# Rotary query rows reach main memory in whole tiles and are put in order there; head sums, head outputs and loads change their places

## The chip, the cores and the metric

One core of a Trainium2 chip runs the whole program. The metric is the device time of one execution in microseconds, taken over repeated executions (median). The profile shown is of one further execution.

## What is computed

Two layers of an encoder for 1024 positions of width 1024, float32. Each layer has, side by side, multi-head latent attention (8 heads, 64 plain and 32 rotary dimensions per query and key, values of 64) and a convolution module of 512 channels with 31 taps; then an output product, and a gated feed-forward part with its own short convolution. Cut to what matters:

```python
q = (c_q @ w_uq[l]).reshape(b, s, MLA_HEADS, MLA_NOPE_DIM + MLA_ROPE_DIM)
q_rope = _apply_rope(q[..., MLA_NOPE_DIM:], cos_h, sin_h)
sc = einsum("bqhd,bkhd->bhqk", qn, k_nope) + einsum("bqhr,bkr->bhqk", qr, k_rope)
p = softmax(sc * scale); o = einsum("bhqk,bkhd->bqhd", p, v)
u = silu(layernorm(dwconv(a * sigmoid(gt))))
x = x + concat([y_attn, u]) @ w_o[l]
x = x + (silu(zg) * zv) @ w_down[l]
```

## The kernel before

Everything lies transposed: features on the 128 partitions, the 1024 positions along the free axis. Numbers are held as pairs (an upper and a lower part), so that a product is three matmuls or, for the scores, matmuls over stacked parts in 16-bit floats.

`project` (L564) makes latents, keys and queries of one layer. TensorE's order is the list `seq`; each section's eviction is a generator, and a small model of the clock (`work`, `launch`, `finish`) decides where its steps are placed on VectorE and ScalarE. Rotary queries come out as two tiles of 128 rows (8 heads by 16 rows): i = 0 the first halves, i = 1 the second halves, each split in an upper part p = 0 and a lower part p = 1 (`query_rope`, L772). Head 0 (`DIRECT`) gets its rows straight from there, by transfers within on-chip memory. The other heads go through main memory: `qd` and `kd` hold plain queries and keys, `qrd` and `krd` the rotary ones, `qrd[p, h]` being the 32 rows of one head in order. `query_rope` appends its spills to the list `spills` (L797), 16 rows and one part each; `query` (L799) empties the list on SyncE's queue from the second block of heads on, with its own spill of `qd` at the end.

`load_head` (L782) loads a head's three tiles by twelve transfers on SyncE's queue: `q` (plain rows, then rotary rows twice), `k` (both parts, the upper part again, the rotary rows), and `qc`, four copies of the lower rotary rows, in a tile that two heads share. `key` (L755) does the same for head 0's keys.

`attention` (L1795) goes over 64 query tiles n = 8 h + qt, two at a time (a pair; the loop at L2059). In each pair TensorE makes products of probabilities and values (`products`, `values`, L1894), the scores of the next pair (`begin`, `scores`, L1825: four matmuls over plain and rotary parts at L1836, and four small ones with `qc` at L1843), and transposes of the present pair's probabilities (`turn`, L1873; the evictions are `upper` on ScalarE and `lower` on VectorE). VectorE takes the largest score of each row (L1854), ScalarE the exponentials (L1862). The load of head h + 1 is put on the queue in the second pair of head h; that of head 1 in the second pair of head 0.

All other work is in `agenda`, a list per step n that `others(n)` runs: `others(n)` in the middle of a pair, `others(n + 1)` at its end. There are the convolution taps on GpSimd (`tap_late`, L2133: a product, then mostly a transfer that accumulates), the totals of the convolution (`conv_total`, from step `TOTAL_TIME` = 57), loads of the output weights (`ahead`: step 55, additions in steps 58 to 61, four more loads in step 61), and the heads' ends. When the last values of a head are through (n = 8 h + 11), the reciprocals of its sums are taken (`inverses`), and `sums` (L1933) is appended to step n + 1: a transpose on TensorE, a copy on ScalarE, and two transfers on SyncE that spread the row over partitions (`rb`). For an odd head `sums` appends the product of the outputs with `rb` on GpSimd (L1944, step 8 h + 10 + `Y_DELAY`) and, `Y_SPLIT` or for head 5 `Y_LAST` steps later, the split of the outputs in two parts (L1946: a cast on ScalarE at L224, a subtraction on GpSimd at L226). Behind the last pair but one `early` (L1959) multiplies these parts with the output weights (L1034), heads 1, 3 and 5 first.

Of the kernel before, what the change touches and what calls it, by code (L numbers as in the profile page):

```python
# [12 lines left out]
F16 = mybir.dt.float16  # L13
# [5 lines left out]
T = 1024  # L19
D = 1024  # L20
DEPTH = 2
HEADS = 8
NOPE = 64
ROPE = 32
HALF = ROPE // 2
# [39 lines left out]
FFN_BANKS = (2, 4)  # L65
SIDE_TIME = 56
TOTAL_TIME = 57
Y_DELAY = 6
Y_LAST = 4
Y_SPLIT = 8  # L70
LATE_FROM = 0
# [70 lines left out]
class Encoder:  # L142
# [421 lines left out]
    def project(self, l, carry):  # L564
# [4 lines left out]
        gates, ckv, kvs, cq, cqs, vs, w = {}, [], [], [], [], [], {}  # L569
        heads, pending, spills = {}, {}, []  # L570
        qd = self.dp.tile([HEADS, NOPE, 2, T], F16, name=f"qd{l}")
        qrd = self.dp.tile([2, HEADS, ROPE, T], F16, name=f"qrd{l}")
        kd = self.dp.tile([HEADS, NOPE, 2, T], F16, name=f"kd{l}")
        krd = self.dp.tile([2, ROPE, T], F16, name=f"krd{l}")
# [4 lines left out]
        st = {}  # L579
# [175 lines left out]
        def key(j):  # L755
            if j == 0:
                heads.update((h, self.head_tiles(l, h)) for h in range(DIRECT))
            p = ps[f"k{j}"]
            hl = self.blk(f"ks{l}_{j}", F16, (128, 2, T))
            nc.scalar.activation(out=hl[:, 0], in_=p, func=AF.Copy, scale=col(6))  # L760
            yield 0.0, 0.0
            nc.vector.scalar_tensor_tensor(out=hl[:, 1], in0=p, scalar=col(6), in1=hl[:, 0], op0=ALU.mult, op1=ALU.subtract)
            self.move(kd[2 * j:2 * j + 2].rearrange("h d p t -> (h d) p t"), hl)
            for h in range(DIRECT if j == 0 else 0):
                k, mine = heads[h][1], hl[h * NOPE:(h + 1) * NOPE]
                for p in range(2):
                    self.move(k[p * NOPE:(p + 1) * NOPE, 0], mine[:, p])
                    self.move(k[NOPE + p * ROPE:NOPE + (p + 1) * ROPE, 1], krd[p])
                self.move(k[0:NOPE, 1], mine[:, 0])
            yield 1.22, 0.0  # L770

        def query_rope(i):  # L772
            p = ps[f"u{i}"]
            c, s = self.blk(f"rc{l}_{i}"), self.blk(f"rs{l}_{i}")
            nc.vector.tensor_tensor(out=c, in0=p, in1=st["cos"], op=ALU.mult)
            nc.vector.tensor_tensor(out=s, in0=p, in1=st["sin"], op=ALU.mult)
            st["rope", i] = c, s
            yield 2.44, 0.0
            if i == 0:
                return  # L780
            (c1, s1), (c2, s2) = st.pop(("rope", 0)), st.pop(("rope", 1))
            nc.vector.tensor_tensor(out=c1, in0=c1, in1=s2, op=ALU.subtract)  # L782
            nc.vector.tensor_tensor(out=c2, in0=c2, in1=s1, op=ALU.add)
            two = [self.blk(f"qr{l}_{i}", F16, (128, 2, T)) for i in range(2)]
            for hl, o in zip(two, (c1, c2)):
                nc.scalar.copy(out=hl[:, 0], in_=o)
            yield 2.5, 1.0
            for i, (hl, o) in enumerate(zip(two, (c1, c2))):
                nc.vector.scalar_tensor_tensor(out=hl[:, 1], in0=o, scalar=1.0, in1=hl[:, 0], op0=ALU.mult, op1=ALU.subtract)
                yield 1.25, 0.0  # L790
                for h in range(DIRECT):
                    for r, (t, p) in enumerate([(heads[h][0][:, 1], 0)] * 2 + [(heads[h][2][:, h % 2], 1)] * 4):
                        at = i * HALF + (NOPE + r * ROPE if p == 0 else (r - 2) * ROPE)
                        self.move(t[at:at + HALF], hl[h * HALF:(h + 1) * HALF, p])
                for p in range(2):
                    for h in range(HEADS):
                        spills.append((qrd[p, h, i * HALF:(i + 1) * HALF], hl[h * HALF:(h + 1) * HALF, p]))  # L797

        def query(j):  # L799
            n = self.blk(f"qn{l}_{j}")  # L800
# [76 lines left out]
        times, starts, t = {}, {}, 0.0  # L877
# [904 lines left out]
    def load_head(self, l, h, qd, qrd, kd, krd, kc):  # L1782
        q, k, qc = tiles = self.head_tiles(l, h)
        self.move(q[0:NOPE], qd[h])
        self.move(q[NOPE:128, 0], qd[h][:, 0])
        for p in range(2):
            self.move(k[p * NOPE:(p + 1) * NOPE, 0], kd[h][:, p])
            self.move(q[NOPE + p * ROPE:NOPE + (p + 1) * ROPE, 1], qrd[0, h])
        self.move(k[0:NOPE, 1], kd[h][:, 0])
        self.move(k[NOPE:128, 1], krd.rearrange("p d t -> (p d) t"))  # L1790
        for r in range(4):
            self.move(qc[r * ROPE:(r + 1) * ROPE, h % 2], qrd[1, h])
        return tiles

    def attention(self, l, u, conv, away, spill, kvs, loaded, ahead, wo, begun):  # L1795
# [4 lines left out]
        state, v, vts = {}, [], {}  # L1800
# [93 lines left out]
        def values(group, c, n):  # L1894
            h, gg = divmod(group, 2)
            st = state[h]
            e = h % 2
            main, aux = slice(e * 64, e * 64 + 64), slice(64 - e * 64, 128 - e * 64)
            if c == 0:
                if gg == 0 and e == 0:  # L1900
                    st["y"], st["rb"] = self.blk(f"yt{l}_{h}"), self.blk(f"rb{l}_{h}")
                elif gg == 0:
                    st["y"], st["rb"] = state[h - 1]["y"], state[h - 1]["rb"]
                st["po", gg] = self.bank(f"o{l}_{h}_{gg}")
            y, rb, po = st["y"], st["rb"], st["po", gg] if c < 3 else st.pop(("po", gg))
            pt = st["pt"][gg][c // 2]
            for i in range(2):
                nc.tensor.matmul(po, v[2 * c + i][:, h // 2, e, :], pt[0][:, 2 * (c % 2) + i, :],  # L1908
                                 start=(c == 0 and i == 0), stop=False, skip_group_check=True)
            if c == 3:  # L1910
                for kt in range(8):
                    rows = slice(kt % 2 * 64, kt % 2 * 64 + 64)
                    nc.tensor.matmul(po[rows], v[kt][:, h // 2, e, main], st["pt"][gg][kt // 4][1][:, kt % 4, :],
                                     start=False, stop=(kt >= 6), skip_group_check=True)
            if c < 3:
                return
            st["pt"].pop(gg)
            qs = HALVES[gg]
            nc.scalar.activation(out=y[main, qs], in_=po[aux, :], func=AF.Copy, scale=vr[aux, 0:1])
            nc.vector.scalar_tensor_tensor(out=y[main, qs], in0=po[main, :], scalar=vr[main, 0:1], in1=y[main, qs], op0=ALU.mult, op1=ALU.add)  # L1920
            if h < HEADS - 2 and gg:
                inverses(h)
                agenda[n + 1].append(lambda: sums(h, main, st, y, rb))
            elif h == HEADS - 1:
                if gg:
                    divide(y[main, qs], main, gg)
                else:
                    agenda[n + 1].append(lambda: (divide(y[main, qs], main, gg), finish(last, y, 0)))
# [46 lines left out]

        ys, inv, po = [], {}, begun["po"]
        total = HEADS * 8
        agenda = defaultdict(list)
        late, rest = [], {j: list(away[j]) for j in range(4)}
        while any(rest.values()):  # L1980
            j = max((j for j in rest if rest[j]), key=lambda j: (all(j != e for e, _ in late[-2:]), len(rest[j]), -j))
# [16 lines left out]
        last = HEADS - 1  # L1998
        state_y = lambda: state[last]["y"]
        agenda[55].append(lambda: inverses(last - 1))  # L2000
        agenda[56].append(lambda: sums(last - 1, slice(0, 64), state[last - 1], state[last - 1]["y"], state[last - 1]["rb"]))
        agenda[60].append(lambda: [self.load_y(l, begun["x"], 0, k) for k in range(2)])
        for c, when in enumerate((60, 62)):
            agenda[when].append(lambda c=c: inv.update({c: inverse(c)}))
# [15 lines left out]
        def products(n):  # L2020
            for g, c in chain.get(n, ()):
                values(g, c, n)
# [35 lines left out]
        others(0)  # L2058
        for pair in range(total // 2 - 1):  # L2059
            n, nxt = 2 * pair + 1, pair + 1  # L2060
            products(n)
            begin(nxt)
            turn(pair, 0)
            upper(pair, 0)
            turn(pair, 1)
            upper(pair, 1)
            largest(2 * nxt)
            ends = [rows(tt) for tt in ROWS_LATE.get(n, ())]
            turn(pair, 3)
            upper(pair, 3)  # L2070
            second.pop(nxt)()
            lower(pair, 0)
            largest(2 * nxt + 1)
            expo(2 * nxt)
            lower(pair, 1)
            for f in ends:
                f()
            others(n)
            products(n + 1)
            ends = [rows(tt) for tt in ROWS_LATE.get(n + 1, ())]  # L2080
            turn(pair, 2)
            upper(pair, 2)
            expo(2 * nxt + 1)
            lower(pair, 2)
            lower(pair, 3)
            for f in ends:
                f()
            others(n + 1)
            for qi in range(2):
                state[pair // 4]["p"].pop(2 * (pair % 4) + qi)  # L2090
# [198 lines left out]
```

## Time and profile before

| | |
|---|---|
| median of 3 runs | 2234.74 us (2232.11 to 2236.47) |
| profiled execution, its own time | 2234.25 us |
| its span | 2232.5 us |
| TensorE busy | 2164.8 us (97%) |
| VectorE, ScalarE, GpSimd busy | 1842.1, 1454.5, 536.4 us |
| DMA | 409.64 MB, mean 183 GB/s |

Times within the profile run from the start of the span. PE is TensorE, PEld its weight loads, DVE VectorE, ACT ScalarE, POOL GpSimd, SP SyncE; a q behind a name is the engine's queue of commands. A row of the waits says who waited, at which line, for whom: the total, the number of times and the longest. A row of a timeline gives start, length (of all instructions merged in it), engine, line, operation, and in brackets the idle time ahead of it. L150 is the helper `move`, which issues most transfers, L1034 and L224 to L226 are helpers too.

### The profile page before, as it was taken

Reading aid. Unit: us, or ns where it says so; the run is one execution under the profiler, and the core shown is the slowest. Engines: PE = TensorE matmul, PEld = TensorE weight load, DVE = VectorE, ACT = ScalarE, POOL = GpSimd, SP = SyncE. Lnnn points to the kernel's source line nnn. Section 1 sums busy time; section 2 is a strip of 40 time slices with the busy share of each in tenths; the row PEclk is TensorE's granted clock in tenths of the full one; section 3 lists DMA queues with packets and bytes.
Section 4 is the critical chain, followed back from the end, with each engine's and each line's share of the span. In section 5 each row is a group of like instructions: output and inputs, shape, how many; then the busy total and the mean of one; then the engine's idle time right before and its main releaser. Section 6 shows DMA issues by size and latency. Waiting matters only on the chain.

```text
span 2232.5 us, 30063 instructions
## 1 busy us (share of the span) xinstructions
PE 2164.8 (97%) x10722; PEld 1243.0 (56%) x10722; DVE 1842.1 (83%) x2531; ACT 1454.5 (65%) x2197; POOL 536.4 (24%) x534
## 2 busy tenths in 40 slices
PE   9999699999999999999999987999999999999998
PEld 8887355664444444644488863557544444446445
DVE  6989588888998887787859785888799988878877
ACT  6365588745888886554623655887558988865554
POOL 1224648401111111000012253583111111110000
PEclk9999899999999999999999998999999999999999
DMA  6897958945588896554568977698456888856533
GB/s 193 185 192 158 230 122 183 279 120 109 131 250 256 225 264 166 188 167 155 168 170 168 206 150 166 138 189 266 131 120 142 242 259 226 249 141 209 183 126 120
DMA packets 173095, 409.64 MB, mean 183 GB/s; under 512 B 24992, under 2 KB 33296, under 8 KB 172944
## 3 DMA queue, kind: packets, MB, share of 16 engines
q0 software_dynamic: 62528, 145.89, 35.9%
q1 hardware_dynamic: 110128, 261.29, 34.9%
q8 instruction: 84, 1.38, 0.3%
q14 instruction: 67, 0.55, 0.1%
q10 hardware_dynamic: 288, 0.53, 0.1%
HBM read 278.35 MB, written 69.66 MB: 156 GB/s over the span
## 4 chain that ended last, share of the span: by engine, by line
PE 86%; ACT 5%; DVE 4%; DMA 3%; issue 2%; SPq 1%; DVEq 0%; ACTq 0%
PE p L1314 35%; PE pd L1559 18%; PE po L1034 7%; PE t L1880 3%; PE pq L242 3%; PE pa L242 3%; ACT p L1862 2%; PE s L1836 2%; PE pkv L242 2%; PE pg L242 2%; PE pg L561 2%; ACT pt L1888 2%; DVE mx L1854 1%; DMA q<-qd 1%; PE o L1908 1%
## 5 line engine op out<-in xcount | busy, mean ns | idle before, releaser
L1314 PE MATMUL p<-b,w 128*128 128x512 f16 x3696 | 800.0, 379 | 0.3
L1314 PEld LDWEIGHTS <-w 128*128 128x128 f16 x3696 | 358.8, 98 | 431.8 <-issue 0.8
L1559 PE MATMUL pd<-ab,wd 128*128 128x512 f16 (+2 forms) x1920 | 404.2, 373 | 0.0
L1204 POOL DMA_DIRECT2D wu<-in_w_up x176 | 152.2, 878 | 766.4 <-DVE w L1278 572.0
L1559 PEld LDWEIGHTS <-wd 128*128 128x128 f16 x1656 | 161.9, 98 | 179.4 <-issue 0.5
L1888 ACT ACTIVATE pt<-t 128x512 f16<-128x512 f32 x256 | 139.6, 597 | 107.3 <-PE t L1880 106.3
L1854 DVE TENSOR_REDUCE mx<-s 128x1 f32<-128x1024 f32 x128 | 155.6, 1216 | 64.3 <-PE s L1843 47.8
L1278 DVE SCALAR_TENSOR_TENSOR w<-wu,wf,w 128x512 f16<-128x512 f32 (+1 forms) x216 | 177.0, 833 | 3.6 <-ACT w L1275 3.6
L1892 DVE SCALAR_TENSOR_TENSOR pt<-t,pt 128x512 f16<-128x512 f32 x256 | 164.4, 681 | 9.1 <-ACT pt L1888 7.9
L1836 PE MATMUL s<-k,q 128*128 128x512 f16 x512 | 134.3, 384 | 31.8 <-DMA k<-kd 26.6
L1275 ACT ACTIVATE w<-wu,wf 128x512 f16<-128x512 f32 (+1 forms) x216 | 164.8, 781 | 0.0
L1862 ACT ACTIVATE p<-s,mx 128x1024 f32<-128x1024 f32 x128 | 142.8, 1116 | 9.6 <-DVE mx L1854 8.6
L1548 ACT ACTIVATE ab<-ac,ds 128x512 f16<-128x512 f32 x108 | 75.5, 717 | 108.5 <-DVE ac L1463 77.7
L2141 POOL TENSOR_SCALAR late<-gate,par 128x1019 f32<-128x1019 f32 (+13 forms) x99 | 134.1, 1354 | 42.8 <-PE pn L242 27.5
L2124 DVE SCALAR_TENSOR_TENSOR conv<-gate,par,conv 128x1009 f32<-128x1009 f32 (+14 forms) x110 | 139.8, 1274 | 3.0 <-ACT conv L656 0.4
L1880 PE MATMUL t<-ident,p 128*128 128x128 f32 x1024 | 140.9, 282 | 0.9 <-DVE pt L1892 0.4
L1880 PEld LDWEIGHTS t<-ident,p 128*128 128x128 f32 x1024 | 116.7, 143 | 31.5 <-issue 13.2
L1774 DVE SCALAR_TENSOR_TENSOR o<-zg,par,o 128x1023 f32<-128x1023 f32 x88 | 112.7, 1280 | 8.9 <-ACT o L1768 7.4
L1322 DVE SCALAR_TENSOR_TENSOR zg<-p,wf,zg 128x512 f32<-128x512 f32 x72 | 54.0, 750 | 71.4 <-PE p L1314 61.7
L1774 DVE SCALAR_TENSOR_TENSOR v<-zv,par,v 128x1023 f32<-128x1023 f32 x88 | 112.1, 1275 | 0.0
L1549 DVE SCALAR_TENSOR_TENSOR ab<-ac,ds,ab 128x512 f16<-128x512 f32 x108 | 79.6, 745 | 19.3 <-ACT ab L1548 19.3
L1836 PEld LDWEIGHTS <-q 128*128 128x128 f16 x512 | 47.6, 98 | 85.0 <-issue 47.4
(2182 smaller groups left out, 3850.8 us busy)
## 6 DMA issues: line engine op xcount, KB each, us to landing
wu<-in_w_up SPq DMA_DIRECT2D x98, 512.0 KB
wu<-in_w_up POOLq DMA_DIRECT2D x176, 256.0 KB, 4.8
sd<-in_w_down SPq DMA_DIRECT2D x44, 512.0 KB
ws<-sd SPq DMA_DIRECT2D x44, 512.0 KB
act<-v SPq DMA_DIRECT2D x36, 512.0 KB
ac<-act SPq DMA_DIRECT2D x72, 256.0 KB
wo<-in_w_o POOLq DMA_DIRECT2D x32, 256.0 KB, 7.6
x_mix<-y SPq DMA_DIRECT2D x32, 256.0 KB
```

The source lines that it names most:

```text
L242: nc.tensor.matmul(ps[:, HALVES[c]], w, x[:, HALVES[c]], start=(k == 0 and s == 0), stop=(k == n - 1 and s == 2))
L1275: nc.scalar.activation(out=t, in_=src, func=AF.Copy, scale=scale[f])
L1278: nc.vector.scalar_tensor_tensor(out=t, in0=src, scalar=scale[f], in1=hi, op0=ALU.mult, op1=ALU.subtract)
L1314: nc.tensor.matmul(ps, w[p][:, k * 128:(k + 1) * 128], b[:, q], start=(i in (1, 5, 2) and k == 0 and t == 0), stop=(k == 3 and t == 2), sk ...
L1559: nc.tensor.matmul(ps[t, m][:, cs], w[i, j][p][:, m * 128:(m + 1) * 128], b[:, q, cs], start=(i in (1, 5, 2) and j == 0 and s == 0), stop= ...
L1774: self.nc.vector.scalar_tensor_tensor(out=o[:, a:b], in0=z[:, at + a:at + b], scalar=self.par[l][:, tap:tap + 1], in1=o[:, a:b], op0=ALU.m ...
L1836: nc.tensor.matmul(two[e][:, cs], q[:, i, at[e]], k[:, i, cs], start=(i == 0 and e == 0), stop=(i == 1 and e == 1), skip_group_check=True)
L1854: nc.vector.tensor_reduce(out=mx, in_=st["s"][qt], op=ALU.max, axis=AX.X, negate=True)
L1862: nc.scalar.activation(out=p, in_=ps, func=AF.Exp, bias=mx, accum_out=st["sums"][:, qt:qt + 1])
L1880: nc.tensor.transpose(tp[:, i, qi * 128:(qi + 1) * 128], st["p"][2 * qp + qi][:, kt * 128:(kt + 1) * 128], self.ident)
L1888: nc.scalar.activation(out=halves(pair, c)[0], in_=tps[pair, c], func=AF.Copy, scale=P_SCALE)
L1892: nc.vector.scalar_tensor_tensor(out=lo, in0=tps.pop((pair, c)), scalar=P_SCALE, in1=hi, op0=ALU.mult, op1=ALU.subtract)
```

## The change

The rotary rows of one i are spilled as one tile of 128 rows with both parts to a new buffer `qrs` in main memory, and two transfers per i put them from there into `qrd`, one for each part. The spills of `query_rope` are six transfers in place of 32. Head 0's rotary keys are loaded by one transfer in place of two. `load_head` issues the same twelve transfers in another order: all query pieces first, then the keys. The loop over r in `query_rope` is written in another way, with the same transfers in the same order. `sums` moves from the list of step n + 1 to a list `ahead_of[n + 2]`, which is run at the start of the pair of that step, ahead of its products. `Y_DELAY` goes from 6 to 7, by which products and splits of the outputs come one step later.

```diff
-Y_DELAY = 6
+Y_DELAY = 7
...
         qd = self.dp.tile([HEADS, NOPE, 2, T], F16, name=f"qd{l}")
+        qrs = self.dp.tile([2, HEADS, HALF, 2, T], F16, name=f"qrs{l}")
         qrd = self.dp.tile([2, HEADS, ROPE, T], F16, name=f"qrd{l}")
...
                 for p in range(2):
                     self.move(k[p * NOPE:(p + 1) * NOPE, 0], mine[:, p])
-                    self.move(k[NOPE + p * ROPE:NOPE + (p + 1) * ROPE, 1], krd[p])
                 self.move(k[0:NOPE, 1], mine[:, 0])
+                self.move(k[NOPE:128, 1], krd.rearrange("p d t -> (p d) t"))
...
                 for h in range(DIRECT):
-                    for r, (t, p) in enumerate([(heads[h][0][:, 1], 0)] * 2 + [(heads[h][2][:, h % 2], 1)] * 4):
-                        at = i * HALF + (NOPE + r * ROPE if p == 0 else (r - 2) * ROPE)
+                    for r in range(6):
+                        p, t = (0, heads[h][0][:, 1]) if r < 2 else (1, heads[h][2][:, h % 2])
+                        at = i * HALF + (NOPE + r * ROPE if r < 2 else (r - 2) * ROPE)
                         self.move(t[at:at + HALF], hl[h * HALF:(h + 1) * HALF, p])
+                spills.append((qrs[i].rearrange("h d p t -> (h d) p t"), hl))
                 for p in range(2):
-                    for h in range(HEADS):
-                        spills.append((qrd[p, h, i * HALF:(i + 1) * HALF], hl[h * HALF:(h + 1) * HALF, p]))
+                    spills.append((qrd[p][:, i * HALF:(i + 1) * HALF], qrs[i][:, :, p]))
...
         self.move(q[0:NOPE], qd[h])
         self.move(q[NOPE:128, 0], qd[h][:, 0])
+        for r in range(2):
+            self.move(q[NOPE + r * ROPE:NOPE + (r + 1) * ROPE, 1], qrd[0, h])
+        for r in range(4):
+            self.move(qc[r * ROPE:(r + 1) * ROPE, h % 2], qrd[1, h])
         for p in range(2):
             self.move(k[p * NOPE:(p + 1) * NOPE, 0], kd[h][:, p])
-            self.move(q[NOPE + p * ROPE:NOPE + (p + 1) * ROPE, 1], qrd[0, h])
         self.move(k[0:NOPE, 1], kd[h][:, 0])
         self.move(k[NOPE:128, 1], krd.rearrange("p d t -> (p d) t"))
-        for r in range(4):
-            self.move(qc[r * ROPE:(r + 1) * ROPE, h % 2], qrd[1, h])
...
             if h < HEADS - 2 and gg:
                 inverses(h)
-                agenda[n + 1].append(lambda: sums(h, main, st, y, rb))
+                ahead_of[n + 2].append(lambda: sums(h, main, st, y, rb))
...
-        agenda = defaultdict(list)
+        agenda, ahead_of = defaultdict(list), defaultdict(list)
...
-        agenda[56].append(lambda: sums(last - 1, slice(0, 64), state[last - 1], state[last - 1]["y"], state[last - 1]["rb"]))
+        ahead_of[57].append(lambda: sums(last - 1, slice(0, 64), state[last - 1], state[last - 1]["y"], state[last - 1]["rb"]))
...
         for pair in range(total // 2 - 1):
             n, nxt = 2 * pair + 1, pair + 1
+            for f in ahead_of.pop(n, ()):
+                f()
             products(n)
             begin(nxt)
```

## Rows read from the trace of the kernel before

**Rows 1.** The page: span, busy time of the engines, and the chain by line.

```profile
span 2232.5 us, 30063 instructions
...
PE 2164.8 (97%) x10722; PEld 1243.0 (56%) x10722; DVE 1842.1 (83%) x2531; ACT 1454.5 (65%) x2197; POOL 536.4 (24%) x534
...
PE p L1314 35%; PE pd L1559 18%; PE po L1034 7%; PE t L1880 3%; PE pq L242 3%; PE pa L242 3%; ACT p L1862 2%; PE s L1836 2%; PE pkv L242 2%; PE pg L242 2%; PE pg L561 2%; ACT pt L1888 2%; DVE mx L1854 1%; DMA q<-qd 1%; PE o L1908 1%
```

**Rows 2.** TensorE's waits: for whom, total us, times, longest us.

```profile
PE s L1836 <- DMA k<-kd: 26.6, 2, 13.7
PE sr L1935 <- DVE pt L1892: 13.8, 12, 1.2
PE s L1843 <- ACT p L1862: 8.2, 20, 2.2
PE s L1836 <- DMA k<-krd: 5.0, 2, 3.2
PE s L1843 <- DMA qc<-qrd: 2.5, 6, 0.6
```

**Rows 3.** TensorE's timeline, layer 0, around the first scores of head 1.

```profile
227.96 1.05 PE L1913 MATMUL o<-pt,v 128*64 128x512 f16 x8
242.72 1.01 PE L1836 MATMUL s<-k,q 128*128 128x512 f16 x2 [13.70 <-DMA k<-kd]
...
249.34 0.60 PE L1843 MATMUL s<-kc,qc 32*128 32x512 f16 x1 [0.34 <-DMA qc<-qrd]
249.87 2.82 PE L1880 MATMUL t<-ident,p 128*128 128x128 f32 x12
```

**Rows 4.** SyncE's queue, layer 0: spills, and load of head 1.

```profile
198.22 23.70 SPq L150 DMA_DIRECT2D qrd<-qr  x32
221.97 4.53 SPq L150 DMA_DIRECT2D qd<-qns  x4
227.31 1.99 SPq L150 DMA_DIRECT2D q<-qd  x2
...
240.79 2.78 SPq L150 DMA_DIRECT2D qc<-qrd  x4
```

**Rows 5.** SyncE's queue, layer 1: the small spills and the first load.

```profile
1301.97 25.98 SPq L150 DMA_DIRECT2D qrd<-qr  x32
...
1333.75 2.29 SPq L150 DMA_DIRECT2D q<-qd  x2
```

**Rows 6.** The chain in order of time: transfers on it, start and length.

```profile
170.87 6.92 DMA kd<-ks
...
227.31 13.46 DMA q<-qd
...
1423.58 2.94 DMA sd<-rs
```

**Rows 7.** Windows: us, engines' busy time, TensorE's granted clock, DMA share, GB/s.

```profile
212.00:216.00 4.00, 3.68 (x24) 2.79 (x23) 3.90 (x7) 3.44 (x8) 3.41 (x5) 1.00 1.07 204
...
244.00:248.00 4.00, 2.03 (x4) 0.33 (x4) 0.00 (x0) 0.00 (x0) 1.70 (x2) 0.50 1.07 231
```

**Rows 8.** TensorE's timeline, layer 0: the transpose of one head's sums.

```profile
396.69 0.27 PE L1935 MATMUL sr<-ident,sums 128*8 128x128 f32 x1 [1.25 <-DVE sums L1931]
396.80 0.59 PE L1908 MATMUL o<-pt,v 128*128 128x512 f16 x2
```

**Rows 9.** ScalarE's timeline, layer 0: the cast of head 5's outputs.

```profile
410.44 1.05 ACT L224 CAST ys_5h<-yt 128x1024 fp32r<-128x1024 f32 x1
```

**Rows 10.** GpSimd's timeline, layer 0: the split of head 5, weight loads.

```profile
412.29 3.00 POOL L226 TENSOR_TENSOR ys_5l<-yt,ys_5h 128x1024 fp32r<-128x1024 f32 x1
...
415.44 2.85 POOL L990 DMA_DIRECT2D wo<-in_w_o  x4
```

**Rows 11.** TensorE's timeline, layer 0: the early output products of head 5.

```profile
417.32 0.39 PE L1034 MATMUL po_e<-ys_5l,wo 128*128 128x512 f32 x1
```

## The prediction

> **What bounds the kernel now.** I read the page first [rows 1]: TensorE is busy for 97% of the span and carries most of the chain that ended last, so only a stretch where TensorE stands still, or an edit that lengthens its work, can move the time. The one entry of that chain that is a transfer of this change is the load of query rows, at 1%. TensorE's waits come next [rows 2]: most of what it waits for stands in one place per layer, the scores of head 1, which wait for keys, rotary keys and rotary queries loaded from main memory; apart from that only the transposes of the heads' sums stand out, with 13.8 us over 12 places.
>
> TensorE's timeline shows the place in layer 0 [rows 3]: the last value products begin at 227.96 us, the scores of head 1 come in pieces from 242.72 on, and the twelve transposes behind them start at 249.87. That is some 20 us almost empty, once per layer. SyncE's queue shows why [rows 4]: 32 small spills of rotary query rows occupy it from 198.22 for 23.70 us, four spills of the other query rows follow, and the first load of head 1 is issued at 227.31. The second layer repeats it with 25.98 us for the 32 [rows 5]. SyncE issues in order, so the load cannot overtake the spills.
>
> The second thing to see is that the transfers themselves are not free in this stretch. The first piece of the load needed 13.46 us to land, and only then the last four pieces could be issued [rows 4, 6]; the windows show the DMA engines full, 1.07 and 1.07, both while the small spills trickle and while the load is under way, and the granted clock of TensorE at 0.50 at the end of the stall, the lower of its two levels [rows 7]. GpSimd's accumulating transfers of convolution taps share those engines. So the stall ends with a queue of transfers, not with the number of instructions on SyncE alone.
>
> **The change, part by part.** The second layer is costed like the first. The sum is made against the profiled execution's own time of 2234.25 us (1.75 more than its span; 0.49 under the median of the three runs).
>
> *Spills.* Per layer 32 transfers of 32 KB go. In their place come, for each half, one whole-tile spill of 512 KB and two transfers of 256 KB from main memory to main memory. These must wait until their whole-tile spill has landed, and SyncE waits in order: behind the first wait stand the second half's spill and its pair, the four other query spills and the load of head 1, which TensorE waits for. So the new chain is: spill, landing, two reorders, spill, landing, two reorders, the first other query spill, load. What a landing costs: 2.94 us for the small sums' spill, 6.92 us for the same-shaped key spill in a full stretch [rows 6]. From 204 us on the engines are as busy as for the latter, so 6.92. What a reorder costs, the trace of before does not show: there is no transfer from main memory to main memory. Below, it is like one of the four big spills, 4.53 / 4 = 1.1 us; above, it costs what the eight small spills took that moved the same rows, 8 x 23.70 / 32 = 5.9 us [rows 4]. The rows are the same 2 KB pieces, so I stay near the upper end. From the first other spill to the first load it was 227.31 - 221.97 = 5.3 us, which I keep.
> - Upper end: 198.2 + 6.9 = 205.1; two reorders to 216.9; the second spill, queued behind them, has landed some 1.1 us later, 218.0; two reorders to 229.8; 5.3 to the load: 235.1, later than before by 7.8 us.
> - Middle: landings of 6.9, reorders of 1.1: 205.1, 207.3, 214.2, 216.4, 221.7: earlier by 5.6 us.
> - Lower end: landings of 2.9 too: 201.1, 203.3, 206.2, 208.4, 213.7: earlier by 13.6 us.
>
> A second estimate does not use the chain: the engines are full, and the change adds 1 MB per layer (the whole-tile spills; the reorders write what the small spills wrote, but must read it from main memory). At the 204 GB/s of the full window [rows 7] that is 5.1 us. I take a load that starts 6.0 us later, between this and the upper end. Here the Trainium skill has a rule that speaks against the change. Its page "DMA: Bandwidth & Descriptors", in the section on why a DMA increments its semaphore by 16, says that a transfer is split over as many of the 16 engines as divide the outermost count of both sides. Eight heads as outermost count would put each reorder on eight engines, for twice the time; by that, the sum goes to the upper end, 2261.9 us, where the rows alone leave everything from 2219 upward open. No row of the trace of before decides it.
>
> *Order within the load.* The twelve pieces stay twelve, but the keys, which the first score matmul needs, now come last, and the four last pieces are issued only once the first have landed, as before [rows 4, 6]. Before, a single 0.60 us matmul was left when the last piece landed [rows 3]. Now a pair of score matmuls at the low clock (1.01 us) and four of 0.5 to 0.6 are left: 3.1 to 3.4 us, some 2.5 us more, on TensorE's path. For the later heads it costs nothing: they are loaded a head ahead. Without that cover each would pay the same 2.5.
>
> *Rotary keys of head 0* load in one piece where there were two: one issue of about 0.7 us less, behind which nothing is due; nothing.
>
> *The transposes of the heads' sums.* Before, they were put last into the list that runs at the end of a pair; now they run first in the next pair. Between those two places no instruction is issued, so TensorE, ScalarE and SyncE (its two transfers included) see the same order. In the trace the transpose already stands right before the next pair's products [rows 8]. Nothing, and the 13.8 us of [rows 2] stay. If I overlooked something, the price lies between those 13.8 us and one such wait of 1.2 us more each time.
>
> *The head outputs one step later* (Y_DELAY). The products and the splits of heads 1, 3 and 5 move by one half pair. The products run on GpSimd, 24% busy; nothing, and some 3 us of GpSimd if its slack were gone. For heads 1 and 3 ScalarE's cast of 1.05 us [rows 9] moves from the end of a pair, where ScalarE waits, to its middle, ahead of an exponential for which TensorE sometimes waits: 0 to 1.05 us each; 0.25 taken, 0.5 per layer. Head 5 is different. Its split now comes in step 61, behind the last weight addition and four weight loads on GpSimd. Before, those loads stood behind the split and were through at 415.44 + 2.85 = 418.3; without its 3.00 us ahead of them they can be through between 415.3 and 418.3, and the split then takes its 3.00 [rows 10]: ready at 418.3 to 421.3. TensorE takes the lower part at 417.32 for the early output products [rows 11]. A stall of 1.0 to 4.0; since the weight addition still waits for its ScalarE copy in step 61, it hardly starts sooner: 3.0 us per layer. TensorE is in order there and its waits behind it are small [rows 2], so it counts fully.
>
> Sum: 2 x (6.0 + 2.5 + 0.5 + 3.0) = 24.0 us, 2258.3 us.
>
> **The rivals.**
> - *The reorders are cheap* (middle case). The stall changes by -5.6 + 2.5 = -3.1 per layer, and 2 x (-3.1 + 3.5) = 0.8 gives 2235.1 us. For it: two big transfers instead of 16 small ones, on a queue whose issue was the slow part [rows 4]. Against it: full engines [rows 7]. 0.18.
> - *Faster:* SyncE's issue was the only limit, landings take 2.9 us, and the load starts 13.6 us earlier: 2 x (-13.6 + 2.5 + 3.5) = -15.2, 2219.1 us. It decides at the second whole-tile spill: if that has landed by 209 us, this case holds. For it: the engines are not yet full right after 198 us. Against it: the first load's own 13.46 us. 0.13.
> - *The sums do move*, and their 13.8 us go: 2244.5 us with the rest as forecast. The order in the code speaks against it. 0.02.
> - *The reorders are dearer still* than the small spills, beyond 2272 us: 0.07.
>
> **How the numbers follow.** The forecast, a longer stall in both layers and a stall at head 5's split, has 0.60 and runs from 2246 (a load 0 to 1 us later, the rest as taken) to 2270 (upper end everywhere, dearest split). With the cheap-reorder case, 2230 to 2242, the range is 2232 to 2270. A measurement tells this kernel from itself to about 0.2%, 4.5 us. Faster by more: the second rival and a trace of the first, 0.15. Within: most of the first rival, 0.13. Slower: the rest, 0.72.
>
> **What would show it.** Right: SyncE's timeline has a long wait between a whole-tile spill and its reorders; the first load of head 1 is issued after 227 us; the transposes after the stall start near 258 instead of 249.87; a new TensorE wait of about 3 us on GpSimd's split of head 5; the waits at the sums' transposes as before. Wrong: the first load issued before 222 us and a shorter wait at the scores of head 1, or no wait at head 5's split. Most of the forecast hangs on the reorders' price; if they land in 1 to 2 us each, it falls.

## The result, and the profile after

The changed kernel takes 2241.08 us (median of 16 runs, 2236.51 to 2247.47) against 2234.76 us of the kernel before (16 runs, 2232.11 to 2237.73): a ratio of 1.0035 [1.0026, 1.0044]. It is slower, as forecast, but by 6.3 us where 24 were forecast (7.8 us by the ratio, which is worked out from all runs and not from the medians); the profiled execution took 2240.83 us.

The page of the changed kernel: span, busy time, chain by line.

```profile
span 2239.1 us, 29984 instructions
...
PE 2162.9 (97%) x10722; PEld 1241.3 (55%) x10722; DVE 1845.9 (82%) x2531; ACT 1455.4 (65%) x2197; POOL 536.8 (24%) x534
...
PE p L1316 35%; PE pd L1561 18%; PE po L1036 7%; PE t L1883 3%; PE pa L242 2%; PE s L1839 2%; ACT p L1865 2%; PE pg L242 2%; DVE conv L2129 2%; PE pg L561 2%; PE pq L242 1%; DMA q<-qd 1%; ACT pt L1891 1%; DVE mx L1857 1%; PE o L1911 1%
```

As in [rows 1], TensorE bounds the kernel, and its 10722 matmuls stand in the same order as before; what differs is the idle time between them and, in places, the granted clock. TensorE's waits in the changed kernel (for whom, total us, times, longest us):

```profile
PE s L1839 <- DMA k<-kd: 33.7, 2, 17.8
PE sr L1938 <- DVE pt L1895: 13.8, 12, 1.2
PE s L1846 <- ACT p L1865: 8.2, 20, 2.2
PE po_e L1036 <- POOL ys_5l L226: 5.5, 2, 2.7
...
PE t L1883 <- DVE pt L1895: 2.2, 6, 0.4
PE s L1839 <- DMA k<-krd: 1.6, 2, 1.4
```

Against [rows 2]: the sums' transposes still wait 13.8 us in 12 places, so their move did nothing. The wait for head 5's split is new: 5.5 us in two places. The wait for keys has grown from 26.6 to 33.7 us, but the other two waits at the same scores shrank: 5.0 to 1.6 us, and 2.5 us to nothing. This wait has changed its name more than its size, as the timelines show. SyncE's queue, changed kernel, layer 0:

```profile
197.65 0.65 SPq L150 DMA_DIRECT2D qrs<-qr  x1
202.01 2.16 SPq L150 DMA_DIRECT2D qrd<-qrs  x2
204.21 0.52 SPq L150 DMA_DIRECT2D qrs<-qr  x1
211.63 1.68 SPq L150 DMA_DIRECT2D qrd<-qrs  x2
213.36 3.78 SPq L150 DMA_DIRECT2D qd<-qns  x4
225.32 1.85 SPq L150 DMA_DIRECT2D q<-qd  x2
```

TensorE's timeline, changed kernel, layer 0, from the last values of head 0 to the first transposes behind the stall:

```profile
227.62 1.05 PE L1916 MATMUL o<-pt,v 128*64 128x512 f16 x8
...
246.49 1.01 PE L1839 MATMUL s<-k,q 128*128 128x512 f16 x2 [17.82 <-DMA k<-kd]
248.86 1.01 PE L1839 MATMUL s<-k,q 128*128 128x512 f16 x2 [1.37 <-DMA k<-krd]
249.81 0.61 PE L1846 MATMUL s<-kc,qc 32*128 32x512 f16 x4
250.35 2.82 PE L1883 MATMUL t<-ident,p 128*128 128x128 f32 x12
```

The load of head 1 is issued at 225.32 where it was 227.31 [rows 4]: 2.0 us earlier. The transposes behind the stall come at 250.35 instead of 249.87 [rows 3]: the stall, counted from the last values, goes from 21.9 to 22.7 us in layer 0. In layer 1 it goes from 22.85 us (1335.44 to 1358.29 before) to 19.7 us:

```profile
1340.63 1.05 PE L1916 MATMUL o<-pt,v 128*64 128x512 f16 x8
1357.55 1.03 PE L1839 MATMUL s<-k,q 128*128 128x512 f16 x2 [15.86 <-DMA k<-kd]
...
1360.32 1.89 PE L1883 MATMUL t<-ident,p 128*128 128x128 f32 x12
```

So the new way of spilling costs nothing on balance. The loss lies at the heads' outputs. GpSimd's timeline, layer 0, and then TensorE's:

```profile
418.41 2.49 POOL L992 DMA_DIRECT2D wo<-in_w_o  x4
420.73 2.53 POOL L226 TENSOR_TENSOR ys_5l<-yt,ys_5h 128x1024 fp32r<-128x1024 f32 x1
```

```profile
420.19 0.39 PE L1036 MATMUL po_e<-ys_5h,wo 128*128 128x512 f32 x1
423.31 0.50 PE L1036 MATMUL po_e<-ys_5l,wo 128*128 128x512 f32 x1 [2.73 <-POOL ys_5l L226]
```

Split and weight loads have changed places [rows 10]; TensorE now waits 2.73 us for the split, and 2.74 us in layer 1. Behind that second wait TensorE's granted clock is also low for a while. Windows of the changed kernel behind the split of layer 0 (first two) and of layer 1 (last two):

```profile
419.00:423.00 4.00, 1.58 (x7) 0.94 (x5) 3.72 (x5) 1.91 (x4) 4.00 (x5) 1.00 1.10 304
423.00:427.00 4.00, 3.69 (x24) 3.25 (x25) 2.64 (x4) 1.09 (x2) 0.26 (x1) 1.00 1.13 347
1527.00:1531.00 4.00, 1.68 (x8) 1.01 (x6) 3.64 (x5) 1.98 (x4) 4.00 (x5) 1.00 1.10 303
1531.00:1535.00 4.00, 3.58 (x15) 3.34 (x16) 1.88 (x3) 1.19 (x2) 0.36 (x1) 0.59 1.13 349
```

The two stalls look alike (TensorE busy 1.58 and 1.68 of 4 us), but only in layer 1 does the clock fall to its lower level, a mean of 0.59 in the window behind. The rest is at the casts of heads 1 and 3. ScalarE's timeline, layer 0:

```profile
330.62 1.13 ACT L1865 ACTIVATE p<-s,mx 128x1024 f32<-128x1024 f32 x1
...
331.71 1.06 ACT L224 CAST ys_1h<-yt 128x1024 fp32r<-128x1024 f32 x1
332.65 0.63 ACT L1891 ACTIVATE pt<-t 128x512 f16<-128x512 f32 x1
333.13 1.14 ACT L1865 ACTIVATE p<-s,mx 128x1024 f32<-128x1024 f32 x1
```

The cast now lies between two exponentials, and ScalarE runs without a gap through it. In the kernel before it lay behind the second of them, ahead of evictions that came later:

```profile
326.50 1.04 ACT L224 CAST ys_1h<-yt 128x1024 fp32r<-128x1024 f32 x1
327.67 1.57 ACT L1888 ACTIVATE pt<-t 128x512 f16<-128x512 f32 x3
```

A part of the cost stands in TensorE's waits: the transposes' wait for VectorE, 2.2 us in six places above, was

```profile
PE t L1880 <- DVE pt L1892: 0.4, 2, 0.2
```

With each TensorE instruction set against its counterpart (start after less start before), the 7.0 us by which the last one is later come together so: load of head 1 +1.45 in layer 0, 0.8 less ahead of it and 4.4 less at it in layer 1, together -3.8; the four casts +0.95, +0.91, +0.88 and +0.90, together +3.6; the two waits for head 5's split +2.69 and +2.76, together +5.5; the low clock behind the second +1.7. The experiments test the load, the casts and the split.

The clock has a share in the load's terms too. Behind the stall TensorE is at the lower level for a while, and there +1.0 us of layer 0 and -1.4 us of layer 1 arise. The 0.8 us ahead of the load in layer 1 are a low clock that only the kernel before has there, behind a wait of 2.18 us for an exponential; its window:

```profile
1317.00:1321.00 4.00, 3.04 (x14) 2.61 (x14) 2.33 (x5) 3.46 (x8) 3.92 (x3) 0.57 1.07 196
```

### The profile page after: what moved, and what is told of

Its sections match the earlier page's. It is cut to its first block, busy times and chain, and to the rows that moved or that the text cites. A ratio compares the mean times of both kernels' runs of the same rounds, so it can differ in the third digit from the quotient of the medians.

```text
span 2239.1 us, 29984 instructions
## 1 busy us (share of the span) xinstructions
PE 2162.9 (97%) x10722; PEld 1241.3 (55%) x10722; DVE 1845.9 (82%) x2531; ACT 1455.4 (65%) x2197; POOL 536.8 (24%) x534
## 4 chain that ended last, share of the span: by engine, by line
PE 81%; DVE 6%; ACT 5%; DMA 5%; issue 2%; SPq 1%; POOL 0%; DVEq 0%; ACTq 0%
PE p L1316 35%; PE pd L1561 18%; PE po L1036 7%; PE t L1883 3%; PE pa L242 2%; PE s L1839 2%; ACT p L1865 2%; PE pg L242 2%; DVE conv L2129 2%; PE pg L561 2%; PE pq L242 1%; DMA q<-qd 1%; ACT pt L1891 1%; DVE mx L1857 1%; PE o L1911 1%
## 5 line engine op out<-in xcount | busy, mean ns | idle before, releaser
L1839 PE MATMUL s<-k,q 128*128 128x512 f16 x512 | 134.7, 386 | 35.6 <-DMA k<-kd 33.7
```

What stands on the lines that cost most here:

```text
L1839: nc.tensor.matmul(two[e][:, cs], q[:, i, at[e]], k[:, i, cs], start=(i == 0 and e == 0), stop=(i == 1 and e == 1), skip_group_check=True)
```

## The experiments

Times are medians. "By ratio" is the ratio to the runs of the kernel before on the same chip, times 2234.76 us, and serves for comparison, since the changed kernel, e1 to e4, e5 to e8 and e9 to e12 each have runs of their own of the kernel before beside them (medians 2234.76, 2234.76, 2236.23 and 2235.50).

| kernel | us | ratio [95%] | by ratio |
|---|---|---|---|
| changed kernel | 2241.08 | 1.0035 [1.0026, 1.0044] | 2242.6 |
| e1 steps only | 2244.49 | 1.0044 [1.0031, 1.0058] | 2244.6 |
| e2 changed, steps undone | 2230.72 | 0.9983 [0.9974, 0.9992] | 2231.0 |
| e3 e2, old load order | 2230.02 | 0.9976 [0.9967, 0.9985] | 2229.4 |
| e4 e2, 16 rows outermost | 2214.72 | 0.9913 [0.9900, 0.9927] | 2215.3 |
| e5 changed, split back | 2234.47 | 0.9992 [0.9983, 1.0002] | 2233.0 |
| e6 e2, four heads each | 2249.79 | 1.0060 [1.0047, 1.0072] | 2248.2 |
| e7 e4, head 1 direct | 2209.78 | 0.9882 [0.9868, 0.9895] | 2208.4 |
| e8 no reorder | 2192.12 | 0.9807 [0.9793, 0.9820] | 2191.6 |
| e9 changed, 16 rows outermost | 2226.24 | 0.9965 [0.9952, 0.9977] | 2226.9 |
| e10 e8, heads aside | 2220.13 | 0.9936 [0.9923, 0.9949] | 2220.5 |
| e11 e8, rows aside | 2211.37 | 0.9894 [0.9880, 0.9908] | 2211.1 |
| e12 e8, steps earlier | 2197.26 | 0.9832 [0.9818, 0.9846] | 2197.2 |

**e1, e2: the two halves of the change apart.** e1 is the kernel before with the step alone; e2 the changed kernel without it.

```diff
 # e1, in the kernel before          # e2, in the changed kernel
-Y_DELAY = 6                         -Y_DELAY = 7
+Y_DELAY = 7                         +Y_DELAY = 6
```

> The kernel before with the head outputs one step later and nothing else (Y_DELAY 7). Theory A (the trace after: the whole loss comes from here): four casts on ScalarE in mid-pair at 0.9 us each and two stalls of 2.7 us at head 5's split, with up to 1.7 us of low clock behind one of them: 9 to 11 us slower than before, 2244 to 2246 us. Theory B (as forecast, the casts nearly hidden): 7 us slower, 2242. Theory C (the loss of the change sits in the spills): within 2 us of before.

> The changed kernel with Y_DELAY back at 6: spills, reorders, order of the loads and sums as changed. Theory A: spills and loads together gain about 3 us over both layers, so 2229 to 2233 us, faster than both kernels. Theory C (as forecast): the stall at head 1 is 8.5 us longer per layer, 2252. A third way: no difference from before, 2235.

e1 is 9.7 us above the kernel before, e2 4.0 below it. So the step costs about 10 us (10.4 between e2 and the changed kernel), and everything else gains 4. TensorE's waits in e1 show the same new row as the changed kernel, without the new spills:

```profile
PE po_e L1034 <- POOL ys_5l L226: 5.5, 2, 2.7
```

**e3: the order within the load.** e2 with the load's order of the kernel before.

```diff
+        for r in range(4):
+            self.move(qc[r * ROPE:(r + 1) * ROPE, h % 2], qrd[1, h])
         return tiles
# and the rotary rows of q between the keys' transfers, as before
```

> As e2_no_step, with the twelve loads of a head in the old order (keys between the queries, the qc pieces last). Theory A (as forecast, the new order costs 2.5 us per layer because the score matmuls all stand behind the last piece): 4 to 5 us under e2_no_step. Theory B: the order is free, since the stall ends with the queue of transfers whatever stands last in it: within 1 us of e2_no_step.

0.7 us less than e2, inside the scatter: the order is free. TensorE then waits 24.3 us for `kd`, 1.6 for `krd` and 3.4 for `qc` instead of 28.7 us for `kd` and 5.6 for `krd`. Whichever piece comes last, the scores end with it.

**e5: the step's own two parts.** The changed kernel, with only the split of head 5 back at its step (`Y_LAST` acts on no other head); the products and the casts of heads 1 and 3 stay a step later.

```diff
-Y_LAST = 4
+Y_LAST = 3
```

> The changed kernel whole, but with the split of heads 5 and 6 put back to step 60 (it waits three steps behind its multiplication in place of four); the casts of the other heads stay one step later. Theory A, from the shift of TensorE's instructions between the two profiles: the split's stall cost 2.7 and 2.8 us in the two layers, and the low clock behind the second another 1.7, so 2233.9 to 2235.6 us, the median of the kernel before, and the 3.6 us of the casts stay paid. Theory B, the wait only changes its place (GpSimd is now late with the multiplication, since it begins it one step later): 2238 to 2242.

By ratio 9.6 us below the changed kernel, by medians 6.6; theory A, and the wait for `ys_5l` is gone from TensorE's waits. What is left above e2, 3.7 us by medians and 2.0 by ratio, is the four casts: TensorE's transposes wait 2.2 us in six places for VectorE as in the changed kernel, and 0.5 us in two in e2. Split and low clock together were measured 7.2 by the shift of instructions.

**e4, e6: the form of the reorder.** The same bytes, with another dimension outermost (e4), or in two transfers of four heads (e6); both on e2. `rows` stands for the 16 rows of one i.

```diff
-spills.append((qrd[p][:, rows], qrs[i][:, :, p]))
# e4
+spills.append((qrd[p][:, rows].rearrange("h d t -> d h t"),
+               qrs[i][:, :, p].rearrange("h d t -> d h t")))
# e6
+for h in range(0, HEADS, 4):
+    spills.append((qrd[p, h:h + 4, rows], qrs[i, h:h + 4, :, p]))
```

> As e2_no_step, with both sides of the reorders written with the 16 rows outermost in place of the 8 heads; the same 128 pieces of 2 KB in each. Theory A (with 8 outermost a reorder keeps only part of the DMA engines busy, and what is queued behind it waits on those): reorders land earlier, the load of head 1 is issued 2 to 3 us earlier per layer, and the time is 4 to 8 us under e2_no_step. Theory B (only the pieces count): the same as e2_no_step within 1.5 us.

> The changed kernel with the steps of the sums as before, and each reorder written as two transfers of four heads in place of one of eight: the same bytes and rows, four more issues a layer. Beside it stand 2230.7 us for reorders of eight heads and 2214.7 for sixteen rows outermost. Theory A, the number of outermost pieces decides over how many engines a transfer is spread, and always the same first ones: four heads lie on four engines, a reorder's bytes take twice as long as with eight, and what was gained from eight to sixteen (8 us a layer) is lost one to two times over: 2240 to 2262. Theory B, two transfers of four heads lie on different engines, or the rows' order within main memory made the difference: 2228 to 2233.

e4 gained 16 us, twice what was expected, and lies below both kernels. e6 lost 19 us by medians and 17 by ratio. Transfers of this stretch (195 to 250 us), with KB of one and the median us from issue to landing; e4 first, then the changed kernel, then e6:

```profile
qd<-qns SPq DMA_DIRECT2D x4, 512.0 KB, 11.7
qrs<-qr SPq DMA_DIRECT2D x2, 512.0 KB, 5.0
```

```profile
qd<-qns SPq DMA_DIRECT2D x4, 512.0 KB, 15.1
qrs<-qr SPq DMA_DIRECT2D x2, 512.0 KB, 7.4
```

```profile
qd<-qns SPq DMA_DIRECT2D x4, 512.0 KB, 22.4
qrs<-qr SPq DMA_DIRECT2D x2, 512.0 KB, 12.6
```

These are not the reorders, but transfers whose form never changed and that stand on the queue behind them (of the two `qrs` the row gives the second, behind the first two reorders: in the changed kernel 204.21 to 211.63). They land the later the fewer pieces the reorder has outermost. Meanwhile the DMA engines were not even full in e6. Its windows (the last two columns are the DMA share and GB/s):

```profile
216.00:220.00 4.00, 3.40 (x24) 2.01 (x22) 3.49 (x7) 3.49 (x8) 3.05 (x3) 1.00 0.90 172
220.00:224.00 4.00, 3.60 (x19) 1.46 (x17) 4.00 (x6) 3.41 (x7) 3.70 (x4) 1.00 0.56 187
```

In the second window the share is 0.56 although the second tile's reorders, issued from 218.01 to 221.44, are under way and the load waits for what is behind them until 238.41: I read it as some engines idle and others with a backlog. The changed kernel had 1.05 and 1.04 in these windows.

The traces' records of single packets, counted by their starts and ends (which overlap a little), bear this out. With a reorder in full flow, e4 has 16.6 of its 2 KB packets in flight on average and no other data (206.0 to 206.5 us). The changed kernel has 8.2, first with 8.2 packets of the spill behind it (206.0 to 206.5), then alone (207.0 to 208.0; the DMA share is 0.46 from 206.5 to 208.0). e6 has 4.2, together with 12.2 of the `qd` spills (224 to 226). Before that, from 220 to 222 us at a share of 0.26, e6 has only 4.2 to 4.9 packets in flight, all of a convolution tap, and none of the reorders already issued. So a reorder had about as many packets in flight as pieces outermost, out of some sixteen in all, and in e6 it waited behind what four of the engines had left over while the others stood empty. The records do not name the engines.

**e9: do the parts add up?** The changed kernel whole, with e4's edit.

> The changed kernel whole (the steps of the sums as in it), with its four reorders a layer written with the sixteen rows outermost in place of the eight heads; nothing else. Theory A, the parts add up: 2241.1 less the 16.0 us that this writing was worth with the other steps, 2225 us, 2222 to 2229. Theory B, the steps of the sums and the load hang together (the cheaper load only uncovers another wait): 2230 to 2238.

They do: the edit is worth 0.0070 of the time here as on e2 (1.0035 to 0.9965, and 0.9983 to 0.9913). With one rewriting of its access the change as a whole would have been faster than the kernel before.

**e7: head 1 not through main memory.** e4 with the constant that says how many heads are filled on the chip.

```diff
-DIRECT = 1
+DIRECT = 2
```

> The kernel with sixteen rows outermost (2214.7 us), and head 1 filled from on-chip memory beside head 0 rather than loaded back from main memory: head 1's load, which TensorE waits for 20.4 us in two layers, leaves the queue, and some 19 small transfers a layer come in ahead of head 0's scores. Theory A: the wait goes and comes back to a part as a later start of head 0, 0 to 6 us a layer: 2194 to 2206. Theory B: the small transfers hold up head 0 (and the spills behind them) by as much as head 1 gains: 2212 to 2225.

5 to 7 us less than e4, between the two theories. The wait at head 1's keys is gone, but head 0 starts 8.3 us later in layer 0 than in the kernel before (209.30 instead of 201.04):

```profile
209.30 1.89 PE L1839 MATMUL s<-k,q 128*128 128x512 f16 x4 [8.50 <-DMA q<-qns]
```

In layer 1 TensorE stands idle for 10.5 us ahead of the same scores.

**e8: no reorder at all.** The whole-tile spill goes to rows that lie interleaved, so that one spill per tile is enough and each head's 32 rows have one distance; the key's rotary rows are interleaved to match, and the products sum over the same rows in another order.

```diff
-qrs = self.dp.tile([2, HEADS, HALF, 2, T], F16, name=f"qrs{l}")
-qrd = self.dp.tile([2, HEADS, ROPE, T], F16, name=f"qrd{l}")
+qrd = self.dp.tile([HEADS, HALF, 2, 2, T], F16, name=f"qrd{l}")
...
-spills.append((qrs[i].rearrange("h d p t -> (h d) p t"), hl))
-for p in range(2):
-    spills.append((qrd[p][:, rows], qrs[i][:, :, p]))
+spills.append((qrd[:, :, i].rearrange("h d p t -> (h d) p t"), hl))
...
-qrd[0, h]
+qrd[h, :, :, 0].rearrange("d i t -> (d i) t")
```

> The kernel with the steps of the sums as before and no reorder at all: each rotary tile is spilled by one transfer into rows that lie interleaved in main memory, each head's load takes its 32 rows from there at every second row, and the key's rotary rows are written interleaved too (one more small transfer a layer; head 0's twelve direct moves write every second partition). The matrix products sum over the same rows in another order. Theory A, the reorders, even over all engines, still hold up what is behind them by their own landings: 3 to 6 us a layer under the kernel with sixteen rows outermost (2214.7): 2203 to 2209. Theory B, with sixteen rows they cost no more than their bytes beside the other transfers: 2210 to 2216. If rows at every second place cost more than they save: above 2216.

2192.12 us, 22.6 under e4 and 43 under the kernel before: well beyond what either theory expected, and the best kernel of this study. SyncE's queue and TensorE's timeline in layer 0:

```profile
198.75 1.37 SPq L150 DMA_DIRECT2D qrd<-qr  x2
200.16 5.11 SPq L150 DMA_DIRECT2D qd<-qns  x4
205.57 2.42 SPq L150 DMA_DIRECT2D q<-qd  x2
```

```profile
228.12 1.05 PE L1914 MATMUL o<-pt,v 128*64 128x512 f16 x8
229.11 1.04 PE L1837 MATMUL s<-k,q 128*128 128x512 f16 x4
```

The load of head 1 is issued at 205.57, and the scores follow the values with no gap. This is the missing scale. Two whole-tile spills in place of 32 small ones are worth 21.7 us of the load's start (227.31 to 205.57); the four reorders take 19.75 of them back (205.57 to 225.32). The change removed a cost and put in another of nearly the same size. And since the whole stall is gone here, the load has slack: the expected 3 to 6 us per layer failed because the stall, with the low clock at its end, can fall to nothing at once (in e4 TensorE still waited 20.4 us for `kd` in the two layers).

**e10, e11: what a reorder's price is made of.** e8, with four transfers of the reorders' shape in their places, from rows of `kd` that landed long before to a place that nobody reads. They do no work for the result.

```diff
+aside = self.dp.tile([2, HEADS, ROPE, T], F16, name=f"as{l}")
...
 spills.append((qrd[:, :, i].rearrange("h d p t -> (h d) p t"), hl))
+for p in range(2):                     # e11: both sides "h d t -> d h t"
+    spills.append((aside[p][:, rows], kd[:, rows, p]))
```

> The kernel without reorders (2192.1 us), and in the place where the reorders stood four transfers a layer of their shape, eight heads of sixteen rows of 2 KB, from rows of keys that landed long before to a place that nothing reads: same bytes, same pieces, but nothing waits for them by data and they wait for no spill. This tells apart what of a reorder's price is the chain of landings and what is the engines it keeps busy. Theory A, the engines: what is behind them on the same engines lands later all the same, 15 to 38 us in the two layers: 2207 to 2230. Theory B, the chain (SyncE standing at a reorder until its spill has landed, the load of head 1 behind that): 2192 to 2198.

> The same with the four transfers aside written with sixteen rows outermost. Theory A, the engines: half of the time on twice as many engines, so a third to a half of what the eight heads cost here: 2196 to 2208. Theory B, the chain: 2192 to 2198, as with eight heads.

e10 costs 28.0 us over e8, e11 19.3. No transfer waits for these by data, so most of the price is not the chain of landings: by ratio 28.8 of 39.3 us (e2 less e8) with eight heads outermost, 19.4 of 23.7 us (e4 less e8) with sixteen rows. I read the larger part of that as the engines they keep busy, since the same bytes with the same number of issues cost 8.8 us less in e11. Some of it is SyncE's issuing, 3.9 us in layer 0 of e10, which no run takes apart. The rest, 10.5 and 4.3 us, is what the real reorders have on top, I think the chain of landings and SyncE standing in it. e11 came out above its range: rows cost two thirds of the heads here, not a third to a half. SyncE's queue in e10, layer 0:

```profile
202.58 1.66 SPq L150 DMA_DIRECT2D as<-kd  x2
204.28 4.50 SPq L150 DMA_DIRECT2D qd<-qns  x4
219.74 1.24 SPq L150 DMA_DIRECT2D q<-qd  x2
```

SyncE never stands before the spills, and still the load, which needs the first of them landed, is issued 15.5 us after it; in e8 it was 5.4.

**e12: a step earlier.** e8 with the heads' outputs one step earlier, the other way from the change.

```diff
-Y_DELAY = 6
+Y_DELAY = 5
```

> The kernel without reorders (2192.1 us), with the multiplications and splits of the head outputs one step earlier than in the kernel before (delay 5), the other way from the change. Theory A, a step later cost 9 to 10 us because casts then lie ahead of exponentials and the last split behind the weight loads; a step earlier has casts in the middle of a pair again, so it costs 2 to 4 us and head 5's split gains nothing: 2193 to 2197. Theory B, each step earlier only helps: 2186 to 2191. If the factors that the multiplication needs are not there in time, GpSimd waits and what is behind it too: above 2198.

5.1 us above e8, a little past the expected 2 to 4. The casts lie between two exponentials again, and that place costs in this direction too; TensorE's wait for exponentials, 7.8 us in e8, has become:

```profile
PE s L1844 <- ACT p L1863: 13.1, 20, 2.2
```

## Why the prediction was right and wrong

- **Direction right, size wrong.** Of the sum 2 x (6.0 + 2.5 + 0.5 + 3.0), the first two terms were wrong, the third too small, the fourth right. They should have read -3.8 us for load and order in both layers together (forecast +17), +3.6 for the casts (forecast +1), +5.5 for the split (forecast +6), and +1.7 for a low clock that had no term. The largest part, 17 of the 24 us, had the wrong sign; the direction came out right by the smaller terms and was in part luck. 2241.08 us lies in the band of the cheap-reorder rival (2230 to 2242), not in the forecast's 2246 to 2270.
- **The step that failed: "a load that starts 6.0 us later".** It started 2.0 us earlier in layer 0 and, against the last values ahead of it, 3.5 us earlier in layer 1 (1.7 us ahead of them before, 5.15 after). The upper end had the reorders in series on SyncE's queue: "205.1; two reorders to 216.9". SyncE did not wait for them. It issued the first two in 2.16 us, and the second whole-tile spill at 204.21, not 216.9. What the forecast charged there, 11.8 us for each pair, came back only in part, and elsewhere: the second spill had SyncE waiting until 211.63, and the load came 12.0 us after the first `qd` spill (213.36 to 225.32), not the 5.3 that the prediction said "I keep". The taken 6.0 lay between a full engine's 5.1 and an upper end of 7.8 that counted as waiting what is overlap.
- **The whole-tile landing, 6.9 taken,** was 3.7 us for the first (issued by 198.30, reorders at 202.01) and 6.9 for the second (204.73 to 211.63; 8.5 in layer 1). The prediction took the engines as full from 204 us on, but in the kernel before their share was 0.63 from 204 to 208 us against 0.98 and 1.08 around the key spill. The rival "faster" was to decide by a second landing at 209: it came at 211.63 with eight heads, and at 209.47 in e4, which is 20 us under the kernel before.
- **"Order within the load", +2.5,** is nothing (e3). The sum took the order's effect from the matmuls left after the last piece, but the wait at the keys and that at `qc` trade against each other.
- **The cheap-reorder rival** was nearer: a load 5.6 us earlier, the stall 3.1 us shorter per layer, 2235.1 us. Of the 7.0 us between the profiles it had 0.8, and missed 2.4 in the load, 2.6 in the casts and 1.7 in the low clock, less 0.5 at the split. Its chain up to the first `qd` spill was too long (216.4 us; it came at 213.36), and the way from there to the load too short (5.3 us; it was 12.0), so that its time was close in part because two errors cancelled.
- **The casts, 0.25 each,** cost 0.9 each, close to the cast's whole 1.05 us [rows 9]: the upper of the prediction's own two bounds. Scores and exponentials form a tight loop here, and an operation laid into it pays for most of its length (0.9 us by the shift of instructions; e5 leaves 2.0 to 3.7 us for the four, and e12 shows the same place cost).
- **The split, 3.0 per layer,** was 2.73 and 2.74, by the mechanism forecast: the weight loads were through at 420.9, and the split stood behind them. The absolute times were off, since all of it lay some 3 us later by then.
- **The sums** cost nothing and gained nothing, as forecast, and so did head 0's rotary keys.
- **The page's rule.** By the Trainium skill's page "DMA: Bandwidth & Descriptors", section on why a DMA increments its semaphore by 16, eight heads outermost confine a reorder to eight engines. The traces agree as far as they show it: 16.6, 8.2 and 4.2 packets of a reorder in flight with sixteen, eight and four pieces outermost. The times agree in order: over no reorder, sixteen rows cost 23.7 us by ratio, eight heads 39.3, four heads 56.5. They do not agree with what the prediction made of it, a total at the upper end, 2261.9 us: that end charges the reorders one after another on SyncE's queue and has the load start at 235.1 us, where it started at 225.32.

What stays open: why the low clock followed one of two like stalls and not the other (in e1, too, it fell behind the second alone, to 0.50 from 1539 to 1543 us, and in e9 behind neither), and how the 21.7 us of the 32 small spills divide into SyncE's issuing and transfers under way.

## What to carry to other kernels

A transfer's price is not its place on the queue: look at what lands late behind it, because four issues of about a microsecond each put the landing behind them off by ten (e10: 15.5 us to the load where e8 had 5.4). When a rewriting of spills moves the time little, price the removed and the added part apart (here 21.7 and 19.75 us of the load's start); the better design keeps the one without the other, as with a layout in main memory that needs no reorder. And an operation moved by one step into a tight loop of two engines costs most of its length (here 0.9 of 1.05 us), though its own engine is busy for only 65% of the span.

## What the runs showed of the hardware beyond that

- The same 256 KB in the same 2 KB pieces, from main memory to main memory, cost 16 us a run less by ratio when the outermost dimension had sixteen pieces than with eight (e4 against e2, and e9 against the changed kernel), and 17 us more in transfers of four (e6). The pieces in flight at once were 16.6, 8.2 and 4.2.
- Spilling to rows that lie 8 KB apart, and loading 2 KB from every 4 KB, brought no wait back: the scores of head 1 in e8 wait for no transfer at all.
- After two stalls of TensorE of 2.73 and 2.74 us at the same place of the program the granted clock stayed at 1.00 in one layer and fell to a mean of 0.59 in the other, which cost 1.7 us. In the kernel before it fell behind a wait of 2.18 us (0.57 from 1317 to 1321 us).
